# Linear attention's levels: differences two by two in place, none for the keys of the last level; later heads' weights get their low parts by a DMA that adds

## The chip, the cores and the metric

The kernel runs on one core of a Trainium2 chip. Work is spread over TensorE (PE, matrix products), VectorE (DVE), ScalarE (ACT), GpSimd (POOL) and the DMA queues, of which before the change SP's alone carries the data. The metric is the device time of one execution in microseconds (us); less is better.

## The reference, cut to what matters

The program is a backbone of two layers over 512 latent tokens and 256 context tokens (768 columns in all, `T`), width 1024. Each layer is a token mixer and a gated convolution MLP; layer 0's mixer is a bidirectional gated linear attention with 4 heads, key width 128 and value width 256, in chunks of 64 tokens:

```python
g = jax.nn.log_sigmoid((h @ a_w1[d]) @ a_w2[d] + a_b[d]) / GLA_GATE_NORM
...
b = jnp.cumsum(gc, axis=2)
b_last = b[:, :, -1:, :]
o_inter = jnp.einsum('bhid,bhde->bhie', qc * jnp.exp(b), s)
diff = jnp.where(mask, b[:, :, :, None, :] - b[:, :, None, :, :], -jnp.inf)
att = jnp.einsum('bhid,bhjd,bhijd->bhij', qc, kc, jnp.exp(diff))
o = o_inter + jnp.einsum('bhij,bhje->bhie', att, vc)
s_new = jnp.exp(b_last)[:, :, 0, :, None] * s + jnp.einsum('bhjd,bhje->bhde', kc * jnp.exp(b_last - b), vc)
```

`g` is the log of a decay for each token and key channel, `b` its running sum within a chunk. This is done forward and backward (over flipped tokens) and the two results are added, normalised, gated by `silu(r)` and projected.

## The kernel before, in words

Tokens lie along the free axis, 128 channels on the partitions; the chunk is 128 tokens here, six chunks (`CH`, `NCH`). A product in full fp32 is made of three faster ones (`mm3`, L294 to L297): both operands are split into a high part (rounded) and a low part (the rest), and low x high, high x low and high x high are added up in PSUM.

**Weights** come in units of 512 KB (`wunit`, L276). A load on SP's queue brings the unit into a staging tile `st` (a pool of three); ScalarE copies it into the high part `wh` (L290), which rounds it; VectorE subtracts for the low part `wl` (L291). `wh` and `wl` lie in a ring of five units. A head of the linear attention uses six: queries, keys, and four of values and gates together (`v` and `r`). A unit's ring place can be written once the matmuls of the unit five before it are done, and `st` is free when both parts are made.

**Decay inside a chunk.** The exponential of a difference of two running sums cannot be split safely into two factors over a whole chunk, so `level` (L560 on) halves the chunk seven times: `s` is 64, 32, ..., 1. Between the two halves of a block of 2s tokens the sum at the border is the reference point. `bF` and `bB` are the forward and backward running sums. L572 to L575 write four differences of half the columns each, one query tile `eq` and one key tile `ek`; L576 and L577 take the exponentials on ScalarE; L578 and L579 multiply by queries and keys; `blocks_of` (L550) makes the matmuls of the level (12 of 64 x 64 for the first, 24 of 32 x 32 for the later ones; the profile counts each twice), and a masked copy on VectorE (L588) or copies on ScalarE (L585) put the result into the attention tile. After the last level POOL copies four blocks (L592). `diag` (L558) is the block's own diagonal, from queries and keys alone.

**A head** has two parts. `part_a` is the first value group, the diagonal, and then the seven levels, with a value group (24 matmuls of 512 columns, `vr_group`) after each of the first five; between them, in heads 0 to 2, come 16 blocks of the modulation's weights (`sa`, 512 KB, two buffers, eight matmuls at L179 each). `part_b` is the decay of keys and queries (L600, L601, L634), their transposes (`kt`, L613), the states (L623, L628) and the outputs: the matmuls of L658, a square with its sum on ScalarE (L662), the root on POOL (`ms` L301, `rs` L303) and a scaled product on VectorE (L664, tiles `xl` and `xc`). Between these steps stand the next head's query and key projections (L515 copies them from PSUM), their rotation (L521 to L525; halves are swapped by small DMAs on SP's queue), and the gates (`gates_z`, `gates_b`: L480 to L496, where `b` is scanned).

**What sets the order.** The program is written head by head; a list scheduler puts each engine's instructions in an order by the place in the text and by modelled costs when the kernel is built. Each engine then runs its own list strictly in order. Tiles of 128 x 768 called `t` (`t3`) come from a pool of six.

Of the kernel before, what the change touches and what calls it, by code (L numbers as in the profile page):

```python
# [9 lines left out]
F32 = mybir.dt.float32  # L10
FR = mybir.dt.float32r
U8 = mybir.dt.uint8
AF = mybir.ActivationFunctionType
OP = mybir.AluOpType
# [6 lines left out]
HEADS = 4  # L21
# [18 lines left out]
def body(ctx, tc, x, ctx_x, small, ada0, ada, w_gla, a_w1, a_w2, w_go, w_fi, w_fo,  # L40
# [232 lines left out]
            o += b - a  # L273
        return out

    def wunit(src, eng=None, scales=None):  # L276


        n = src.shape[-1]
        st = wload(src)  # L280
        ring[0] = (ring[0] + 1) // 2 * 2 % NW
        (a, _), = wspans(2)
        hi, lo = (w[:, a:a + n] for w in WR)
        if scales:
            for i in range(2):
                s_, h_, l_ = (t_.rearrange("p (k i n) -> p k i n", i=2, n=128)[:, :, i, :] for t_ in (st, hi, lo))
                nc.scalar.activation(h_, s_, AF.Copy, scale=scales[i])
                nc.vector.scalar_tensor_tensor(l_, s_, scales[i], h_.bitcast(F32), OP.mult, OP.subtract)
            return hi, lo
        nc.scalar.activation(hi, st, AF.Copy)  # L290
        (eng or nc.vector).tensor_sub(lo, st, hi.bitcast(F32))  # L291
        return hi, lo

    def mm3(out, a, b, first, last, **at):  # L294
# [125 lines left out]

    Q_SCALE = 128.0 ** -0.5
    with tc.tile_pool(name="gla", bufs=6) as pool:
        def t3(dt=F32):
            return pool.tile([128, T], dt, name="t3", tag="t3", bufs=6)

        cosT = pool.tile([128, N_LAT], F32, name="cosT", bufs=1)
        sinT = pool.tile([128, N_LAT], F32, name="sinT", bufs=1)
# [44 lines left out]
        def gates_z(h):  # L472
            st[h]["g"] = []
            for d in range(2):
                e = t3()
                mn = t3()
                bias = sT[:, R_GB + 4 * d + h:R_GB + 4 * d + h + 1]
                for a, b in RNG:
                    ps = ps_aux()
                    mm(ps[:, 0:b - a], aw2[:, d, h * 128:(h + 1) * 128], low[d][:, a:b], start=True, stop=True)  # L480
                    nc.scalar.activation(e[:, a:b], ps[:, 0:b - a], AF.Abs, bias=bias)
                    nc.vector.tensor_scalar(mn[:, a:b], ps[:, 0:b - a], bias, 0.0, OP.add, OP.min)
                st[h]["g"].append((e, mn))
# [14 lines left out]
                st[h]["b"].append(bt)  # L498

        def qk_weights(h, i):  # L500
            st[h]["w", i] = wunit(w_gla[h, i])

        def qk_group(h, i, r):
            nm = "qk"[i]
            if r == 0:
                st[h][nm] = pool.tile([128, T], F32, name=nm, tag=nm, bufs=1)
            dst = st[h][nm]
            a, b = RNG[r]
            if h == 0:
                ps = groups[2 + 2 * i + r][2]  # L510
            else:
                wh, wl = (w.rearrange("p (k n) -> p k n", k=KD) for w in st[h]["w", i])
                ps = ps_mm()
                proj_fm(wh, wl, a, b, ps)
            nc.scalar.activation(dst[:, a:b], ps[:, 0:b - a], AF.Copy, scale=Q_SCALE if i == 0 else 1.0)  # L515

        def rope(h, i):
            dst = st[h]["qk"[i]]
            sw = t3()
            for o in (0, 64):  # L520
                nc.sync.dma_start(sw[o:o + 32, 0:N_LAT], dst[o + 32:o + 64, N_CTX:])  # L521
                nc.sync.dma_start(sw[o + 32:o + 64, 0:N_LAT], dst[o:o + 32, N_CTX:])
            nc.vector.tensor_mul(sw[:, 0:N_LAT], sw[:, 0:N_LAT], sinT)
            nc.vector.tensor_mul(dst[:, N_CTX:], dst[:, N_CTX:], cosT)
            nc.vector.tensor_add(dst[:, N_CTX:], dst[:, N_CTX:], sw[:, 0:N_LAT])  # L525

        def vr_weights(h, q):
            st[h]["wv", q] = wunit(w_gla[h, 2 + q])

        def vr_group(h, t):  # L530
            if h == 0:
# [28 lines left out]
        def level(h, li):  # L560
            s = LEVELS[li]
            n = T // (2 * s)
            bF, bB = st[h]["b"]

            def v(t_):
                return t_.rearrange("p (n two s) -> p n two s", two=2, s=s)

            cF = v(bF)[:, :, 0, s - 1:s].to_broadcast([128, n, s])
            cB = v(bB)[:, :, 1, 0:1].to_broadcast([128, n, s])
            eq = t3()  # L570
            ek = t3()
            nc.vector.tensor_sub(v(eq)[:, :, 1, :], v(bF)[:, :, 1, :], cF)  # L572
            nc.vector.tensor_sub(v(eq)[:, :, 0, :], v(bB)[:, :, 0, :], cB)
            nc.vector.tensor_sub(v(ek)[:, :, 0, :], v(bF)[:, :, 0, :], cF)
            nc.vector.tensor_sub(v(ek)[:, :, 1, :], v(bB)[:, :, 1, :], cB)  # L575
            nc.scalar.activation(eq, eq, AF.Exp, scale=1.0 / GATE)  # L576
            nc.scalar.activation(ek, ek, AF.Exp, scale=-1.0 / GATE)  # L577
            nc.vector.tensor_mul(eq, eq, st[h]["q"])  # L578
            nc.vector.tensor_mul(ek, ek, st[h]["k"])  # L579
            att, attd = st[h]["att"], st[h]["attd"]  # L580
            if s >= 32:
                ps = blocks_of(ek, eq, s, 1)
                for j in range(CH // s):
                    i = s * (j ^ 1)
                    nc.scalar.activation(att[s * j:s * j + s, :, i:i + s], ps[s * j:s * j + s], AF.Copy)  # L585
            else:
                ps = blocks_of(ek, eq, 32, 0)
                nc.vector.copy_predicated(attd, lvl[:, li - 2:li - 1, :].to_broadcast([128, NCH, 32]), ps)  # L588
            if s == 1:
                for j in range(4):  # L590
                    p_ = slice(32 * j, 32 * j + 32)
                    nc.gpsimd.tensor_copy(att[p_, :, p_], attd[p_])  # L592

        def key_decay(h, d):
            bt = st[h]["b"][d]
            last = ch(bt)[:, :, CH - 1:CH] if d == 0 else ch(bt)[:, :, 0:1]
            ed = sml.tile([128, NCH, 1], F32, name=f"ed{d}", tag=f"ed{d}", bufs=2)
            exps.append(nc.scalar.activation(ed, last, AF.Exp, scale=1.0 / GATE))
            kd = t3()
            nc.vector.tensor_sub(ch(kd), ch(bt), last.to_broadcast([128, NCH, CH]))  # L600
            exps.append(nc.scalar.activation(kd, kd, AF.Exp, scale=-1.0 / GATE))  # L601
            nc.vector.tensor_mul(kd, kd, st[h]["k"])
            st[h]["kd", d] = kd
            st[h]["ed", d] = ed

        def key_turn(h, d):
            kd = st[h].pop(("kd", d))
            kt = t3()
            for c0, c1 in ((0, 4), (4, 6)):
                ps = ps_aux()  # L610
                for c in range(c0, c1):
                    nc.tensor.transpose(ps[:, (c - c0) * CH:(c - c0 + 1) * CH], kd[:, c * CH:(c + 1) * CH], ident)
                nc.scalar.activation(kt[:, c0 * CH:c1 * CH], ps[:, 0:(c1 - c0) * CH], AF.Copy)  # L613
            st[h]["kt", d] = kt
            st[h]["S", d] = {}
# [13 lines left out]
            S[order[i + 1]] = s_new  # L629

        def query_decay(h):
            for d in range(2):
                e = t3()
                exps.append(nc.scalar.activation(e, st[h]["b"][d], AF.Exp, scale=1.0 / GATE))  # L634
                nc.vector.tensor_mul(e, e, st[h]["q"])
                st[h]["qd", d] = e
# [48 lines left out]
        def part_a(h, extra=None):  # L685
            vr_group(h, 0)
            diag(h)
            for i in range(7):
                level(h, i)
                todo = ada_step(pool, *blocks.pop(0)) if blocks and i < 6 else None  # L690
                if i < 5:
                    vr_group(h, i + 1)
                if todo:
                    todo()
                if extra and i >= 5:
                    extra(i - 5)

        def part_b(h, fill):

# [35 lines left out]
        def chain(*fs):  # L735
            def f():
                for g in fs:
                    g()
            return f
# [25 lines left out]
        for h in range(HEADS):  # L765
            part_a(h, turn_early if h == HEADS - 1 else None)
            n = h + 1
            if n < HEADS:
                qk_weights(n, 0)
                qk_weights(n, 1)  # L770
                part_b(h, [lambda: qk_group(n, 0, 0),
                           lambda: qk_group(n, 0, 1),
                           chain(lambda: rope(n, 0), lambda: qk_group(n, 1, 0)),
                           lambda: qk_group(n, 1, 1),
                           chain(lambda: rope(n, 1), lambda: gates_z(n)),
                           chain(lambda: gates_b(n), *[lambda q=q: vr_weights(n, q) for q in range(4)])])
            else:
                part_b(h, [lambda i=i: turn_early(i) for i in range(2, 7)])
        for t in (2, 3, 4, 5, 0, 1):
# [699 lines left out]
```

## Time and profile before

| | before |
|---|---|
| time, median of 3 runs | 1696.29 us (1695.89 to 1698.62) |
| profiled execution, its own time | 1698.42 us |
| span of the profiled execution | 1696.6 us |
| TensorE busy | 1643.0 us, 97% of the span |
| VectorE busy | 1173.5 us, 69% |
| ScalarE busy | 721.2 us, 43% |
| POOL busy | 175.0 us, 10% |
| mean granted TensorE clock | 0.994 of full speed |
| moved on SP's DMA queue | 177.97 MB |

Times in the views are us from the start of the span, durations ns. A row of a group has the source line, the engine, the operation, output and inputs, shapes, how many, then busy us and mean ns, then the idle time in front and what ended it. A row of waits has the waiting engine and line, what it waited for, and then us in total, times, and the longest. The linear attention takes about 80 to 392 us of the span.

### The profile page before, as it was taken

To read this page: it belongs to the slowest core of one execution; us is meant where nothing else is said; L and a number is where in the kernel's file an instruction comes from. 1 tells how busy PE (TensorE), PEld (TensorE's weight loads), DVE (VectorE), ACT (ScalarE), POOL (GpSimd) and SP (SyncE) were. 2 spreads that over 40 slices of the span, in tenths; PEclk is the share of its full clock that TensorE was granted. 3 is DMA by queue.
4 is the path that set the end of the run, shared out by engine and by line. 5 is a ranking of instruction groups with operands and counts; after the bars stand their busy time and mean duration, and the time that the engine had idled before them with its cause. 6 is when DMAs were issued, how large, how long until landed. Compare 5 with 4: busy or idle time off the path is not lost.

```text
span 1696.6 us, 27006 instructions
## 1 busy us (share of the span) xinstructions
PE 1643.0 (97%) x10867; PEld 1410.7 (83%) x10867; DVE 1173.5 (69%) x1949; ACT 721.2 (43%) x1265; POOL 175.0 (10%) x297
## 2 busy tenths in 40 slices
PE   5999999999999999999999999999998999999997
PEld 3768878778899998999999788888887888888887
DVE  4797777865997876978767665666668755555555
ACT  3655645553753343433425454434344422222232
POOL 1001010110000000000000043433332000000000
PEclk9999999999999999999999999999999999999999
DMA  7653523014233332524223043434331323322321
GB/s 268 189 176 100 175 75 107 20 51 144 93 125 112 112 112 75 163 74 146 78 87 100 1 132 93 126 112 131 95 114 53 95 92 100 98 89 75 112 88 50
DMA packets 54190, 179.70 MB, mean 106 GB/s; under 512 B 7024, under 2 KB 10864, under 8 KB 54064
## 3 DMA queue, kind: packets, MB, share of 16 engines
q1 hardware_dynamic: 54064, 177.97, 33.0%
q8 instruction: 85, 1.39, 0.3%
q14 instruction: 41, 0.34, 0.1%
HBM read 173.75 MB, written 2.10 MB: 104 GB/s over the span
## 4 chain that ended last, share of the span: by engine, by line
PE 84%; DVE 6%; ACT 4%; DMA 3%; issue 1%; POOL 1%; SPq 0%; POOLq 0%; DVEq 0%; ACTq 0%
PE mm L295 17%; PE mm L296 16%; PE mm L297 16%; PE aux L295 8%; PE aux L297 8%; PE aux L296 8%; PE mm L1259 2%; PE aux L1242 2%; DMA sa<-in 2%; PE aux L1217 2%; PE aux L658 1%; PE aux L623 1%; DMA st<-in 1%; PE aux L179 1%; PE mm L154 1%
## 5 line engine op out<-in xcount | busy, mean ns | idle before, releaser
L295 PE MATMUL mm<-hh,wl 128*128 128x512 f32 (+3 forms) x864 | 307.0, 358 | 5.0 <-ACT hh L379 2.5
L296 PE MATMUL mm<-hl,wh 128*128 128x512 f32 (+3 forms) x864 | 302.0, 350 | 0.3 <-DVE hl L308 0.3
L297 PE MATMUL mm<-hh,wh 128*128 128x512 f32 (+3 forms) x864 | 301.7, 350 | 0.0
L296 PE MATMUL mm<-ul,wh 128*128 128x512 f32 (+1 forms) x544 | 189.3, 348 | 0.3 <-DVE ul L308 0.3
L297 PE MATMUL mm<-uh,wh 128*128 128x512 f32 (+1 forms) x544 | 189.5, 349 | 0.0
L295 PE MATMUL mm<-uh,wl 128*128 128x512 f32 (+1 forms) x544 | 189.4, 350 | 0.0
L295 PEld LDWEIGHTS mm<-hh,wl 128*128 128x128 f32 (+1 forms) x864 | 162.8, 189 | 28.9 <-issue 5.1
L291 DVE TENSOR_TENSOR wl<-st,wh 128x1024 fp32r<-128x1024 f32 (+1 forms) x126 | 153.2, 1221 | 45.9 <-ACT wh L290 45.5
L290 ACT ACTIVATE wh<-st 128x1024 fp32r<-128x1024 f32 (+1 forms) x127 | 132.1, 1053 | 121.6 <-issue 69.6
L319 DVE SCALAR_TENSOR_TENSOR xl<-mm,mod,xl 128x512 f32<-128x512 f32 (+1 forms) x168 | 116.2, 698 | 95.0 <-PE mm L297 94.5
L296 PEld LDWEIGHTS mm<-hl,wh 128*128 128x128 f32 (+1 forms) x864 | 163.5, 189 | 18.4 <-issue 0.8
L297 PEld LDWEIGHTS mm<-hh,wh 128*128 128x128 f32 (+1 forms) x864 | 163.2, 189 | 18.3 <-issue 0.8
L295 PE MATMUL aux<-hh,wl 128*128 128x384 f32 (+2 forms) x496 | 174.0, 351 | 0.0
L296 PE MATMUL aux<-hl,wh 128*128 128x384 f32 (+2 forms) x496 | 173.7, 350 | 0.0
L297 PE MATMUL aux<-hh,wh 128*128 128x384 f32 (+2 forms) x496 | 173.7, 350 | 0.0
L270 ACT ACTIVATE wh<-st 128x512 fp32r<-128x512 f32 (+1 forms) x126 | 94.3, 756 | 165.9 <-issue 57.0
L295 PEld LDWEIGHTS mm<-uh,wl 128*128 128x128 f32 x544 | 103.0, 190 | 15.9 <-ACT uh L307 2.4
L296 PEld LDWEIGHTS mm<-ul,wh 128*128 128x128 f32 x544 | 103.2, 190 | 14.9 <-DVE ul L308 0.5
L271 DVE TENSOR_TENSOR wl<-st,wh 128x512 fp32r<-128x512 f32 (+1 forms) x126 | 104.6, 849 | 14.4 <-ACT wh L270 13.9
L297 PEld LDWEIGHTS mm<-uh,wh 128*128 128x128 f32 x544 | 103.0, 189 | 13.4
L355 POOL TENSOR_TENSOR rs<-ms,mhalf 128x2 f32<-128x2 f32 (+1 forms) x10 | 10.0, 1003 | 934.2 <-DVE ms L353 934.2
L295 PEld LDWEIGHTS aux<-hh,wl 128*128 128x128 f32 x496 | 93.7, 189 | 8.7 <-issue 1.4
(319 smaller groups left out, 3172.1 us busy)
## 6 DMA issues: line engine op xcount, KB each, us to landing
st<-in SPq DMA_DIRECT2D x201, 512.0 KB, 3.7
sa<-in SPq DMA_DIRECT2D x98, 512.0 KB, 3.7
sx<-in SPq DMA_DIRECT2D x14, 512.0 KB, 7.0
xl<-in SPq DMA_DIRECT2D x8, 512.0 KB, 5.8
xc<-in SPq DMA_DIRECT2D x4, 512.0 KB, 7.8
out<-y SPq DMA_DIRECT2D x16, 128.0 KB, 1.7
raw<-in SPq DMA_DIRECT2D x16, 96.0 KB, 2.5
t<-q SPq DMA_DIRECT2D x16, 64.0 KB, 2.0
```

The source lines that it names most:

```text
L154: mm(ps[32 * j:32 * j + 32, 256 * m:256 * m + 256], cs[:, 4 * half + j, :], st[:, j, :], start=half == 0, stop=half == 1, skip_group_check ...
L270: nc.scalar.activation(hi, s_, AF.Copy)
L271: nc.vector.tensor_sub(lo, s_, hi.bitcast(F32))
L290: nc.scalar.activation(hi, st, AF.Copy)
L291: (eng or nc.vector).tensor_sub(lo, st, hi.bitcast(F32))
L295: mm(out, a[1], b[0], start=first, stop=False, **at)
L296: mm(out, a[0], b[1], start=False, stop=False, **at)
L297: mm(out, a[0], b[0], start=False, stop=last, **at)
L319: nc.vector.scalar_tensor_tensor(x_, ps, gate(l, n, d, rng), x_, OP.mult, OP.add)
L1217: mm(pss[hh][:, off:off + 256], qe[a_][p_, 128 * t:128 * t + 128], ke[b_][p_, ks], start=i == 0, stop=i == 2)
L1242: nc.tensor.transpose(pT[:, i * 128:(i + 1) * 128], S2[:, o:o + 128], ident)
L1259: mm(po[64 * hh:64 * hh + 64, 128 * t:128 * t + 128], V[:, vs[i], 64 * hh:64 * hh + 64], PTs[hh][:, i * 128:(i + 1) * 128], start=i == 0, ...
```

## The change

Four edits, all of them in layer 0's linear attention:

1. Tiles of 128 x 768 are taken in pairs (`pair`): one tile of 128 x 1536, three buffers in place of six. The two halves are freed together.
2. In `level` the query and key tiles are the halves of one pair. For s above 1 one instruction writes both differences against the forward border (the second half of each block of `eq`, the first half of each block of `ek`), one both against the backward border: two of 768 columns for four of 384. For s = 1 a block's key is its own reference, so the key tile is `k` itself: no difference, exponential or product of keys.
3. For heads 1 to 3 the low part is made in another way: ScalarE copies `-st` into `wl` with rounding, and then a DMA on POOL's queue reads the weight again from memory and adds it to `wl`. Head 0 keeps the subtraction.
4. The next head's query and key weights are called for inside `part_a` (after the first and the sixth level) and not behind it; the four value units one by one in the first four gaps of `part_b`, and not all in the sixth.

```diff
--- before.py
+++ after.py
@@ -273,7 +273,7 @@
             o += b - a
         return out
 
-    def wunit(src, eng=None, scales=None):
+    def wunit(src, eng=None, scales=None, added=False):
 
 
         n = src.shape[-1]
@@ -288,7 +288,11 @@
                 nc.vector.scalar_tensor_tensor(l_, s_, scales[i], h_.bitcast(F32), OP.mult, OP.subtract)
             return hi, lo
         nc.scalar.activation(hi, st, AF.Copy)
-        (eng or nc.vector).tensor_sub(lo, st, hi.bitcast(F32))
+        if added:
+            nc.scalar.activation(lo, st, AF.Copy, scale=-1.0)
+            nc.gpsimd.dma_start(lo, src, accum_op=OP.add)
+        else:
+            (eng or nc.vector).tensor_sub(lo, st, hi.bitcast(F32))
         return hi, lo
 
     def mm3(out, a, b, first, last, **at):
@@ -420,8 +424,10 @@
 
     Q_SCALE = 128.0 ** -0.5
     with tc.tile_pool(name="gla", bufs=6) as pool:
-        def t3(dt=F32):
-            return pool.tile([128, T], dt, name="t3", tag="t3", bufs=6)
+        def pair():
+
+            t_ = pool.tile([128, 2 * T], F32, name="t2", tag="t2", bufs=3)
+            return t_, t_[:, 0:T], t_[:, T:2 * T]
 
         cosT = pool.tile([128, N_LAT], F32, name="cosT", bufs=1)
         sinT = pool.tile([128, N_LAT], F32, name="sinT", bufs=1)
@@ -472,8 +478,7 @@
         def gates_z(h):
             st[h]["g"] = []
             for d in range(2):
-                e = t3()
-                mn = t3()
+                _, e, mn = pair()
                 bias = sT[:, R_GB + 4 * d + h:R_GB + 4 * d + h + 1]
                 for a, b in RNG:
                     ps = ps_aux()
@@ -498,7 +503,7 @@
                 st[h]["b"].append(bt)
 
         def qk_weights(h, i):
-            st[h]["w", i] = wunit(w_gla[h, i])
+            st[h]["w", i] = wunit(w_gla[h, i], added=h > 0)
 
         def qk_group(h, i, r):
             nm = "qk"[i]
@@ -516,7 +521,9 @@
 
         def rope(h, i):
             dst = st[h]["qk"[i]]
-            sw = t3()
+            if i == 0:
+                st[h]["sw"] = pair()
+            sw = st[h]["sw"][1 + i]
             for o in (0, 64):
                 nc.sync.dma_start(sw[o:o + 32, 0:N_LAT], dst[o + 32:o + 64, N_CTX:])
                 nc.sync.dma_start(sw[o + 32:o + 64, 0:N_LAT], dst[o:o + 32, N_CTX:])
@@ -525,7 +532,7 @@
             nc.vector.tensor_add(dst[:, N_CTX:], dst[:, N_CTX:], sw[:, 0:N_LAT])
 
         def vr_weights(h, q):
-            st[h]["wv", q] = wunit(w_gla[h, 2 + q])
+            st[h]["wv", q] = wunit(w_gla[h, 2 + q], added=h > 0)
 
         def vr_group(h, t):
             if h == 0:
@@ -565,18 +572,23 @@
             def v(t_):
                 return t_.rearrange("p (n two s) -> p n two s", two=2, s=s)
 
-            cF = v(bF)[:, :, 0, s - 1:s].to_broadcast([128, n, s])
-            cB = v(bB)[:, :, 1, 0:1].to_broadcast([128, n, s])
-            eq = t3()
-            ek = t3()
-            nc.vector.tensor_sub(v(eq)[:, :, 1, :], v(bF)[:, :, 1, :], cF)
-            nc.vector.tensor_sub(v(eq)[:, :, 0, :], v(bB)[:, :, 0, :], cB)
-            nc.vector.tensor_sub(v(ek)[:, :, 0, :], v(bF)[:, :, 0, :], cF)
-            nc.vector.tensor_sub(v(ek)[:, :, 1, :], v(bB)[:, :, 1, :], cB)
+            cF, cB = v(bF)[:, :, 0, s - 1:s], v(bB)[:, :, 1, 0:1]
+            both, eq, ek = pair()
+            if s == 1:
+                nc.vector.tensor_sub(v(eq)[:, :, 1, :], v(bF)[:, :, 1, :], cF)
+                nc.vector.tensor_sub(v(eq)[:, :, 0, :], v(bB)[:, :, 0, :], cB)
+                ek = st[h]["k"]
+            else:
+
+
+                for c_, bt, first, second in ((cF, bF, T, s), (cB, bB, 0, T + s)):
+                    halves = bass.AP(both.tensor, both.offset + first,
+                                     [list(both.ap[0]), [2 * s, n], [second - first, 2], [1, s]])
+                    nc.vector.tensor_sub(halves, v(bt), c_[:, :, :, None].to_broadcast([128, n, 2, s]))
+                nc.scalar.activation(ek, ek, AF.Exp, scale=-1.0 / GATE)
+                nc.vector.tensor_mul(ek, ek, st[h]["k"])
             nc.scalar.activation(eq, eq, AF.Exp, scale=1.0 / GATE)
-            nc.scalar.activation(ek, ek, AF.Exp, scale=-1.0 / GATE)
             nc.vector.tensor_mul(eq, eq, st[h]["q"])
-            nc.vector.tensor_mul(ek, ek, st[h]["k"])
             att, attd = st[h]["att"], st[h]["attd"]
             if s >= 32:
                 ps = blocks_of(ek, eq, s, 1)
@@ -596,7 +608,9 @@
             last = ch(bt)[:, :, CH - 1:CH] if d == 0 else ch(bt)[:, :, 0:1]
             ed = sml.tile([128, NCH, 1], F32, name=f"ed{d}", tag=f"ed{d}", bufs=2)
             exps.append(nc.scalar.activation(ed, last, AF.Exp, scale=1.0 / GATE))
-            kd = t3()
+            if d == 0:
+                st[h]["kds"] = pair()
+            kd = st[h]["kds"][1 + d]
             nc.vector.tensor_sub(ch(kd), ch(bt), last.to_broadcast([128, NCH, CH]))
             exps.append(nc.scalar.activation(kd, kd, AF.Exp, scale=-1.0 / GATE))
             nc.vector.tensor_mul(kd, kd, st[h]["k"])
@@ -605,7 +619,9 @@
 
         def key_turn(h, d):
             kd = st[h].pop(("kd", d))
-            kt = t3()
+            if d == 0:
+                st[h]["kts"] = pair()
+            kt = st[h]["kts"][1 + d]
             for c0, c1 in ((0, 4), (4, 6)):
                 ps = ps_aux()
                 for c in range(c0, c1):
@@ -629,8 +645,9 @@
             S[order[i + 1]] = s_new
 
         def query_decay(h):
+            qds = pair()
             for d in range(2):
-                e = t3()
+                e = qds[1 + d]
                 exps.append(nc.scalar.activation(e, st[h]["b"][d], AF.Exp, scale=1.0 / GATE))
                 nc.vector.tensor_mul(e, e, st[h]["q"])
                 st[h]["qd", d] = e
@@ -694,6 +711,8 @@
                     todo()
                 if extra and i >= 5:
                     extra(i - 5)
+                if h < HEADS - 1 and i in (0, 5):
+                    qk_weights(h + 1, i // 5)
 
         def part_b(h, fill):
 
@@ -766,14 +785,12 @@
             part_a(h, turn_early if h == HEADS - 1 else None)
             n = h + 1
             if n < HEADS:
-                qk_weights(n, 0)
-                qk_weights(n, 1)
-                part_b(h, [lambda: qk_group(n, 0, 0),
-                           lambda: qk_group(n, 0, 1),
-                           chain(lambda: rope(n, 0), lambda: qk_group(n, 1, 0)),
-                           lambda: qk_group(n, 1, 1),
+                part_b(h, [chain(lambda: qk_group(n, 0, 0), lambda: vr_weights(n, 0)),
+                           chain(lambda: qk_group(n, 0, 1), lambda: vr_weights(n, 1)),
+                           chain(lambda: rope(n, 0), lambda: qk_group(n, 1, 0), lambda: vr_weights(n, 2)),
+                           chain(lambda: qk_group(n, 1, 1), lambda: vr_weights(n, 3)),
                            chain(lambda: rope(n, 1), lambda: gates_z(n)),
-                           chain(lambda: gates_b(n), *[lambda q=q: vr_weights(n, q) for q in range(4)])])
+                           lambda: gates_b(n)])
             else:
                 part_b(h, [lambda i=i: turn_early(i) for i in range(2, 7)])
         for t in (2, 3, 4, 5, 0, 1):
```

In the order of TensorE at head 2's first level (L550 in the old text, L557 in the new) the rows before are, from the queries' and keys' diagonal on, with the matmuls of the first value group between:

```order
L550 MATMUL aux<-q,k 32x32 x24
...
L297 MATMUL mm<-wh,hh 128x512
L550 MATMUL aux<-t_2469,t_2470 64x64 x12
L179 MATMUL aux<-sa,cs 32x256 x8
L295 MATMUL mm<-wh,hl 128x512
```

and now:

```order
L557 MATMUL aux<-q,k 32x32 x24
...
L299 MATMUL mm<-wh,hl 128x512
L557 MATMUL aux<-t_2420 64x64 x12
L179 MATMUL aux<-sa,cs 32x256 x8
L557 MATMUL aux<-t_2488 32x32 x24
L300 MATMUL mm<-wl,hh 128x512
```

The second level follows on the first. Counted from the last gate projection (`low`), 51 value matmuls stood before the 64 x 64 ones in head 2 and 61 stand there now; in head 1 it was 48 and is 60, in head 3 52 and 59, in head 0 68 and 75.

In the order of VectorE at the same place (head 2; `b_...` are the two running sums, `t_2469` and `t_2470` the first level's query and key tiles, `t_2535` the second level's) the rows before are:

```order
L558 TENSOR_TENSOR attd<-aux,two_i 128x192
L572 TENSOR_TENSOR t_2469<-b_2365 128x6x64
L573 TENSOR_TENSOR t_2469<-b_2370 128x6x64
L574 TENSOR_TENSOR t_2470<-b_2365 128x6x64
L575 TENSOR_TENSOR t_2470<-b_2370 128x6x64
L572 TENSOR_TENSOR t_2535<-b_2365 128x12x32
L578 TENSOR_TENSOR t_2469<-t_2469,q 128x768
L579 TENSOR_TENSOR t_2470<-t_2470,k 128x768
L573 TENSOR_TENSOR t_2535<-b_2370 128x12x32
```

and now, where `t_2420` and `t_2488` are the first and the second level's pairs:

```order
L565 TENSOR_TENSOR attd<-aux,two_i 128x192
L587 TENSOR_TENSOR t_2420<-b_2332 128x6x2x64
L587 TENSOR_TENSOR t_2420<-b_2337 128x6x2x64
L587 TENSOR_TENSOR t_2488<-b_2332 128x12x2x32
L587 TENSOR_TENSOR t_2488<-b_2337 128x12x2x32
L589 TENSOR_TENSOR t_2420<-t_2420,k 128x768
L591 TENSOR_TENSOR t_2420<-t_2420,q 128x768
L589 TENSOR_TENSOR t_2488<-t_2488,k 128x768
L591 TENSOR_TENSOR t_2488<-t_2488,q 128x768
```

Both differences of the second level now stand ahead of the first level's products; it was one of four.

In POOL's list between the attention tile's copies of head 0 and the outputs of that head stood:

```order
L592 COPY att<-attd 32x6x32 x4
L301 TENSOR_SCALAR ms<-ss 128x1
L303 TENSOR_TENSOR rs<-ms,mhalf 128x1
```

and now:

```order
L293 DMA wl<-in 128x1024 x3
L604 COPY att<-attd 32x6x32 x4
L293 DMA wl<-in 128x1024 x2
L305 TENSOR_SCALAR ms<-ss 128x1
L307 TENSOR_TENSOR rs<-ms,mhalf 128x1
L293 DMA wl<-in 128x1024
```

Adding transfers for the next head stand ahead of these copies and between the pairs of the root.

## The prediction

> **What bounds the kernel now.** I first read the page's totals, then the table of windows over the linear attention (roughly 80 to 392 us; the rest of the program keeps its instructions in order), then what TensorE waits for there.
>
> ```profile
> span 1696.6 us, 27006 instructions
> PE 1643.0 (97%) x10867; PEld 1410.7 (83%) x10867; DVE 1173.5 (69%) x1949; ACT 721.2 (43%) x1265; POOL 175.0 (10%) x297
> ```
>
> ```profile
> 100.00:120.00 20.00, 18.29 (x295) 10.94 (x293) 16.97 (x29) 10.14 (x15) 0.00 (x0) 1.00 0.71 216
> ...
> 200.00:220.00 20.00, 19.85 (x158) 18.85 (x157) 7.76 (x15) 10.61 (x23) 2.95 (x8) 1.00 0.48 152
> ...
> 240.00:260.00 20.00, 17.18 (x217) 11.26 (x216) 19.38 (x36) 11.80 (x21) 0.00 (x0) 1.00 0.42 132
> ...
> 320.00:340.00 20.00, 19.14 (x238) 14.95 (x237) 20.00 (x37) 12.64 (x23) 0.00 (x0) 1.00 0.01 2
> ```
>
> Each row gives a stretch's ends and length, the busy us of TensorE, its weight loads, VectorE, ScalarE and POOL with their instructions, TensorE's granted clock, the DMA engines' busy share and GB/s. TensorE sets the end. VectorE is full while a head's seven levels run (19.38 and 20.00 of 20 us), and still TensorE is at 17 to 19 us there; where the next head is projected VectorE has 12 us in 20 to spare. VectorE work is worth something only where TensorE waits for it:
>
> ```profile
> PE aux L179 <- DMA sa<-in: 3.5, 6, 1.4
> PE aux L550 <- DVE t L579: 2.9, 3, 1.1
> PE aux L671 <- DVE xl L664: 1.4, 2, 0.7
> PE aux L623 <- DVE xl L664: 1.2, 3, 0.4
> PE aux L550 <- DVE k L525: 1.0, 1, 1.0
> PE aux L658 <- DVE xl L664: 1.0, 2, 0.5
> PE aux L671 <- DVE xc L664: 0.5, 1, 0.5
> PE aux L623 <- ACT t L613: 0.3, 1, 0.3
> ```
>
> These are all of TensorE's waits between 80 and 392 us, 11.8 us in sum: 3.5 for the modulation weights `sa`, 8.3 for VectorE and ScalarE. That caps any gain from this change near 12 us, 0.7% of the time. The three waits on L579 are the first level of heads 1, 2 and 3; later levels wait for nothing, since a value group stands between them on TensorE.
>
> **The change part by part.** *Fewer instructions on VectorE.* The prices:
>
> ```profile
> L579 DVE TENSOR_TENSOR t<-t,k 128x768 f32<-128x768 f32 x28 | 26.8, 956 | 1.1 <-ACT t L577 1.0
> ...
> L577 ACT ACTIVATE t<-t 128x768 f32<-128x768 f32 x28 | 23.7, 846 | 4.2 <-DVE t L575 3.1
> ...
> L291 DVE TENSOR_TENSOR wl<-st,wh 128x1024 fp32r<-128x1024 f32 x18 | 21.8, 1224 | 16.0 <-ACT wh L290 15.6
> ...
> L290 ACT ACTIVATE wh<-st 128x1024 fp32r<-128x1024 f32 x18 | 19.0, 1066 | 4.2 <-PE mm L297 2.5 <-DMA st<-in 1.7
> ...
> L600 DVE TENSOR_TENSOR t<-b 128x768 f32<-128x768 f32 x8 | 7.4, 952 | 0.0
> ```
>
> The timeline of VectorE at head 1's first level shows that these durations overlap by about 0.08 us, so the distance from start to start is the real cost:
>
> ```profile
> 163.21 0.35 DVE L558 TENSOR_TENSOR attd<-aux,two_i 128x192 f32<-128x192 f32 x1
> 163.47 0.55 DVE L573 TENSOR_TENSOR t<-b 128x384 f32<-128x384 f32 x1
> 163.93 0.56 DVE L574 TENSOR_TENSOR t<-b 128x384 f32<-128x384 f32 x1
> 164.40 0.55 DVE L575 TENSOR_TENSOR t<-b 128x384 f32<-128x384 f32 x1
> 164.87 0.55 DVE L572 TENSOR_TENSOR t<-b 128x384 f32<-128x384 f32 x1
> 165.34 0.95 DVE L578 TENSOR_TENSOR t<-t,q 128x768 f32<-128x768 f32 x1
> 166.21 0.95 DVE L579 TENSOR_TENSOR t<-t,k 128x768 f32<-128x768 f32 x1
> ```
>
> A half-width difference costs 0.47 us, a full-width operation 0.87. The new differences are 768 wide with a broadcast operand, like L600, so 0.87 each is my value; were their four-dimensional pattern to cost nothing extra or as much as the two halves it replaces, the bounds are 0.87 and 0.94. Six levels of a head go from 4 x 0.47 = 1.88 to 2 x 0.87 = 1.74, which is only 0.14 us each; the last level loses 2 x 0.47 + 0.87 = 1.81 and one exponential of 0.85 on ScalarE. For four heads: 24 x 0.14 + 4 x 1.81 = 10.6 us. The 18 differences of the weights' low parts take away 18 x 1.14 = 20.5 more. About 31 us leave VectorE, but nearly all under cover of TensorE's own work: the weights' part lies where VectorE was idle, the levels' part behind the first level, where TensorE does not wait. If that cover were gone, those 31 us would count; the cap above says it is not.
>
> *The first level of heads 1 to 3.* Here two things move. The order now has 60, 61 and 59 value-projection matmuls between a head's gate projection and its first level's matmuls, where it had 48, 51 and 52: 12, 10 and 7 more in front, and in head 1 seven more modulation ones. One stands 0.23 us behind the other:
>
> ```profile
> 164.35 0.39 PE L296 MATMUL mm<-wl,hh 128*128 128x512 f32 x1
> 164.58 0.39 PE L297 MATMUL mm<-wh,hh 128*128 128x512 f32 x1
> ...
> 165.58 0.62 PE L179 MATMUL aux<-sa,cs 128*32 128x256 f32 x2
> 167.22 0.92 PE L550 MATMUL aux<-t,t 128*64 128x64 f32 x24 [1.02 <-DVE t L579]
> ```
>
> So TensorE comes to the first level about 2.8, 2.3 and 1.6 us later (that only moves work it has to do anyhow). On VectorE the first level's chain gets longer, though: between the diagonal and the second product there stand two (head 1: one) full-width differences of its own, two of the *next* level's, and two products. In head 1 that is 0.26 + 5 x 0.87 + 0.08 = 4.7 us from L558 to the end, against 167.16 - 163.21 = 3.95; in heads 2 and 3 it is 5.6 against 4.4 (one half-width difference more than head 1 had). The waits shrink by the differences, as far as they last: all of head 1's 1.0 (2.8 - 0.7 leaves 2.1), 1.1 in head 2 (2.3 - 1.2) and 0.4 in head 3 (1.6 - 1.2). Sum **-2.5 us**, bounds -2.9 (all three waits) and 0: ScalarE puts two copies of a finished value group (0.4 us each) and one weight pass ahead of head 1's gates, which could eat head 1's part.
>
> *ScalarE.* It gets 18 more passes over a weight at L290's price, 18 x 1.06 = 19.1 us, and loses 4 x 0.85: +15.7 us. ScalarE is at 10 to 13 us of 20 in the windows above, so this fits; what counts is who queues behind. In each of heads 0 to 2 one pass stands ahead of the second key copy and waits for the same projection, so keys, their rotation swap and the copies behind come 1.06 us later. The output chain (square on ScalarE, root on POOL, L664 on VectorE) is what 4.1 us of the waits above end on. A pass ahead of such a square would cost up to 1.06 us, in three heads 3.2. Against that VectorE reaches L664 sooner, having no 1.14 us difference in front of it. I take **+0.5 us**, from -1 to +3.
>
> *The adding DMAs.* 18 transfers of 512 KB go out on POOL's queue. No row shows such a transfer; the nearest are loads of the same size:
>
> ```profile
> st<-in SPq DMA_DIRECT2D x201, 512.0 KB, 3.7
> ...
> xc<-in SPq DMA_DIRECT2D x4, 512.0 KB, 7.8
> ```
>
> An add reads a source and its destination and writes once; 3.7 to 7.8 us bounds it, and I take 6. What must be met, in head 2 on the clock of before:
>
> ```profile
> 206.13 1.09 ACT L290 ACTIVATE wh<-st 128x1024 fp32r<-128x1024 f32 x1
> ...
> 211.26 1.05 ACT L290 ACTIVATE wh<-st 128x1024 fp32r<-128x1024 f32 x1
> 225.71 0.40 PE L296 MATMUL mm<-wl,hh 128*128 128x512 f32 x1
> ...
> 230.54 0.40 PE L296 MATMUL mm<-wl,hh 128*128 128x512 f32 x1
> ```
>
> The middle value weights have high parts at 207 and 212; with one more pass each the adds leave by about 208 and 214, and the first low part is needed at 225.7, the third one's around 230.5. That leaves 16 us for one transfer and some 6 us each if four run one after the other, so I cost this at **0**. The cover is the key projection; without it each head would wait the whole transfer, 3 x 6 = 18 us. On POOL four copies of the attention tile and the ms/rs pairs queue behind adds that wait for ScalarE's pass; the copies are needed some 10 us after they are made, an ms/rs pair at once (in the 0.5 above). [...]
>
> *Modulation weights in head 0.* Their loads go round two buffers, and the chain that ended last runs through them:
>
> ```profile
> 99.67 5.41 DMA sa<-in
> ...
> 105.82 3.88 DMA sa<-in
> ...
> 110.44 4.49 DMA sa<-in
> ...
> 115.68 4.47 DMA sa<-in
> ```
>
> A buffer is asked for again only when TensorE has used it. In the new order the first use stands 7 value matmuls later (1.6 us), with two weight loads ahead of the ring on SP's queue. The ring takes the same time after that, with 1.6 us less work to fill it: **+1.2 us**, bounds 0 (head 0 was not late everywhere) and +3 (a load of 3.7 us in between). The paired tiles use the same memory; released two by two they cost 0 unless a stage waits for a pair, bound 1 us.
>
> Sum: -2.5 + 0.5 + 0 + 1.2 = -0.8 us on the profiled execution's 1698.42, and an estimated -1 (one 1.14 us difference) where L664 and the state updates no longer queue behind weight differences in gaps that the view does not name: **-1.8 us**, 1696.6 on that execution. It lies 2.1 us above the median of the three, 1696.29, so on the median the forecast is **1694.5 us**: within 0.2% (3.4 us), which is about what a measurement of this kernel can tell from no change.
>
> **Rivals.** *All VectorE waits go* (0.37): the seven kinds of wait other than `sa` end, 8.3 us: 1688.0, or enough of them to come under 1692.9. For it: VectorE is relieved at every place named. Against: the L664 waits end on POOL's root, which nothing shortens.
>
> *The ring takes the whole gain* (counted with the forecast's 0.42): -2.5 + 3 gives 1696.8; the change then does what it says and moves only which wait ends last.
>
> *The adds come late* (0.14, slower): each of heads 1 to 3 starts its value group on a low part that has not landed. It decides from 16 us for one or 6 us each in a row. At 8 us each, from 208 on, the third lands at 232, 1.5 us late, and the fourth at 240, needed another 4.8 us after the third (as far apart as 225.7 and 230.5): 4.7 late. Some 3 us per head: 1694.5 + 9 = 1703.5. For it: 0.71 of the DMA engines' time is taken in 100 to 120 us. Against: 0.48 where head 2 is fed.
>
> [...]
>
> **Numbers.** Forecast with the ring 0.42, all waits gone 0.37, late adds 0.14, descriptors 0.07. Faster by over 0.2% (below 1692.9): 0.37. Within 0.2% (1692.9 to 1699.7): 0.42. Slower, the last two cases: 0.21. The likeliest case's own range is 1692.9 to 1698; to hold 8 in 10 it must reach most of the second case and the start of the slow ones: 1686 to 1701.
>
> **What would show it.** In the profile after: L550's waits on the second product under 1 us in sum (step one); the new differences at 0.95 us, 0.87 apart; ScalarE about 16 us busier; TensorE's wait for `sa` up by 1 to 2 us; no wait of L295 or L296 on a DMA at the start of a head's value group. I am wrong if TensorE waits there for a low part, if its sum of waits between 80 and 392 us falls under 6 us (more gain) or rises over 15 (a loss), or if the part after 400 us moves.

## The result and the profile after

The changed kernel takes **1715.49 us** (median of 5, 1712.07 to 1716.69) where the kernel before, on the same chip, takes 1696.29: ratio **1.0103**, 95% interval 1.0092 to 1.0114. It is slower by 1%, where 1694.5 us was predicted. The profiled execution took 1712.07 us.

The page of the changed kernel, its totals, DMA queues and DMA issues (size of one, median us from issue to landing):

```profile
span 1710.3 us, 26970 instructions
PE 1647.9 (96%) x10867; PEld 1409.8 (82%) x10867; DVE 1142.3 (67%) x1871; ACT 731.1 (43%) x1279; POOL 188.3 (11%) x315
...
q1 hardware_dynamic: 54064, 177.97, 31.9%
q0 software_dynamic: 2592, 9.44, 3.0%
...
st<-in SPq DMA_DIRECT2D x201, 512.0 KB, 3.7
...
wl<-in POOLq DMA_DIRECT2D x18, 512.0 KB, 7.8
```

VectorE lost 31.2 us (1173.5 to 1142.3), just what was worked out, and yet the profiled execution got 13.7 us longer than the one before (19.2 by the medians). What TensorE waited for most in the linear attention, now 80 to 410 us:

```profile
PE aux L179 <- DMA sa<-in: 6.6, 7, 3.7
PE aux L485 <- DVE xc L681: 2.6, 2, 2.0
PE aux L557 <- DVE t L591: 2.3, 3, 1.0
PE aux L639 <- DVE xl L681: 2.1, 3, 0.9
PE aux L485 <- DVE S L644: 1.9, 3, 1.0
```

All its waits there come to 20.2 us, where they were 11.8; the prediction had named over 15 as a sign that it is wrong. No value-group matmul waits for a low part: the adding transfers are in time for their own readers. Instead modulation weights come 3.7 us late once, and the gate projection (L485) waits for VectorE, which it never did before. Where this happens shows in the chain of waits between 104 and 154 us (start, us, what):

```profile
106.85 4.33 DMA sa<-in
...
111.93 7.50 DMA sa<-in
119.43 0.04 issue
119.48 1.08 PE aux L179 x8
...
141.41 8.89 DMA t<-q
```

and what POOL did then, in its timeline:

```profile
111.93 0.87 POOL L293 DMA_DIRECT2D wl<-in  x1 [28.42 <-ACT wl L292]
118.40 0.86 POOL L293 DMA_DIRECT2D wl<-in  x1 [5.60 <-ACT wl L292]
...
136.16 0.86 POOL L293 DMA_DIRECT2D wl<-in  x1 [6.68 <-ACT wl L292]
138.04 0.86 POOL L293 DMA_DIRECT2D wl<-in  x1 [1.02 <-ACT wl L292]
```

An adding transfer is issued and a modulation load starts in the same hundredth of a microsecond, 111.93, and the load takes 7.5 us where those before it in the ring take 4.3 to 4.8. At 136 to 142 us three more adds go out with weight loads, and a swap of 64 KB, 2.0 us before, lands after 8.9 us. VectorE, in order, stands at the rotation (L530) and behind it wait the output's scaling (L681) and the states (L644), whose PSUM buffers the gate projection needs.

There is a second cost behind these two stalls. Two windows of the changed kernel, columns as in the prediction, then its TensorE timeline around the two pauses:

```profile
120.00:140.00 20.00, 19.87 (x208) 16.96 (x201) 4.40 (x7) 15.97 (x29) 4.57 (x8) 0.93 0.63 182
140.00:160.00 20.00, 17.43 (x80) 15.25 (x79) 6.45 (x12) 3.83 (x7) 3.10 (x5) 0.91 0.83 205
```

```profile
119.48 1.08 PE L179 MATMUL aux<-sa,cs 128*32 128x256 f32 x8 [3.69 <-DMA sa<-in]
...
121.51 0.63 PE L301 MATMUL mm<-wh,hh 128*128 128x512 f32 x1
121.93 0.63 PE L299 MATMUL mm<-wh,hl 128*128 128x512 f32 x1
...
152.17 0.45 PE L485 MATMUL aux<-low,aw 96*128 96x384 f32 x1 [2.03 <-DVE xc L681]
153.16 0.44 PE L485 MATMUL aux<-low,aw 96*128 96x384 f32 x1 [0.54 <-DVE S L644]
...
155.29 0.63 PE L300 MATMUL mm<-wl,hh 128*128 128x512 f32 x1
155.72 0.63 PE L301 MATMUL mm<-wh,hh 128*128 128x512 f32 x1
```

Behind both pauses the matmuls stand 0.42 to 0.43 us apart, not 0.23, for about 3 us; the granted clock of the two windows is 0.93 and 0.91 (1.00 before). That is up to 20 x 0.07 + 20 x 0.09 = 3.2 us.

By head, from its first 64 x 64 matmul to the next head's, the changed kernel needs 87.3, 79.7 and 79.9 us; without the adding transfers and with nearly the same order on TensorE (the second run below) it is 77.4, 77.7 and 79.0. So 9.9 of the loss lie between the first levels of heads 0 and 1, 2.0 and 0.9 behind. Of the 9.9, 5.5 are named waits (9.2 in sum against 3.7) and some 3 the slow clock; about 1 us has no name.

### The profile page after: what moved, and what is told of

Its sections match the earlier page's. It is cut to its first block, busy times and chain, and to the rows that moved or that the text cites. A ratio compares the mean times of both kernels' runs of the same rounds, so it can differ in the third digit from the quotient of the medians.

```text
span 1710.3 us, 26970 instructions
## 1 busy us (share of the span) xinstructions
PE 1647.9 (96%) x10867; PEld 1409.8 (82%) x10867; DVE 1142.3 (67%) x1871; ACT 731.1 (43%) x1279; POOL 188.3 (11%) x315
## 3 DMA queue, kind: packets, MB, share of 16 engines
q1 hardware_dynamic: 54064, 177.97, 31.9%
## 4 chain that ended last, share of the span: by engine, by line
PE 76%; DVE 8%; ACT 6%; DMA 6%; issue 2%; POOL 1%; SPq 1%; POOLq 0%; DVEq 0%; ACTq 0%
PE mm L299 15%; PE mm L301 15%; PE mm L300 15%; PE aux L299 7%; PE aux L301 7%; PE aux L300 7%; DMA sa<-in 2%; PE mm L1276 2%; PE aux L1259 2%; PE aux L1234 2%; DMA t<-q 1%; DMA st<-in 1%; ACT wh L290 1%; PE aux L675 1%; DVE wl L271 1%
## 5 line engine op out<-in xcount | busy, mean ns | idle before, releaser
L295 DVE TENSOR_TENSOR wl<-st,wh 128x1024 fp32r<-128x1024 f32 (+1 forms) x108 | 132.0, 1227 | 28.8 <-ACT wh L290 28.3
```

## The experiments

Each ratio is against runs of the kernel before on the same chip in the same session (medians 1698.5 to 1699.2 us there).

**e1: the same instructions, an eighth of the bytes.**

```diff
-            nc.gpsimd.dma_start(lo, src, accum_op=OP.add)
+            nc.gpsimd.dma_start(lo[:, 0:128], src[:, 0:128], accum_op=OP.add)
```

> The changed kernel with every instruction and every engine's order kept, but each adding transfer carries 128 of its 1024 columns (64 KB, not 512 KB); the rest of the low part stays the negated weight, so the weights of heads 1 to 3 are computed wrong and only the time counts. Theory traffic (the 512 KB adding transfers take DMA engine time from the modulation loads in head 0 and from the 64 KB rotation swaps, whose landing went from 2.0 to 8.4 us): the 7.5 us load and the 8.9 us swap go back to about 4.5 and 2 us, TensorE's waits in 95 to 160 us fall by 6 to 9 us, and the time is 1697 to 1703. Theory ScalarE and order (the 18 extra passes ahead of the query copies, and the new order): nothing of that leaves, 1710 to 1716.

1702.65 us, ratio 1.0024 (1.0012 to 1.0037): three quarters of the loss are gone with the bytes alone, the order of the engines unchanged but for two neighbouring matmuls on TensorE. In its waits and DMA issues between 80 and 410 us:

```profile
PE aux L179 <- DMA sa<-in: 5.0, 11, 1.1
```

```profile
wl<-in POOLq DMA_DIRECT2D x18, 64.0 KB, 4.9
...
t<-q SPq DMA_DIRECT2D x12, 64.0 KB, 5.6
```

No wait is over 1.1 us and none is left at the gate projection. The swaps did not go back to 2 us, though: on SP's queue two weight loads now stand right ahead of them, perhaps since `st` comes free later with ScalarE's second pass (not tested). At 5.6 us they do no harm.

**e2: no adding transfers at all**; the low parts come from VectorE, everything else as changed.

```diff
-            st[h]["w", i] = wunit(w_gla[h, i], added=h > 0)
+            st[h]["w", i] = wunit(w_gla[h, i])
...
-            st[h]["wv", q] = wunit(w_gla[h, 2 + q], added=h > 0)
+            st[h]["wv", q] = wunit(w_gla[h, 2 + q])
```

> The changed kernel with the low parts of all heads by VectorE's subtraction again; pairs, levels and the new place of the weights stay. Traffic or ScalarE at fault: 1692 to 1698. Order at fault (weights called for earlier, value matmuls ahead of the first level): 1706 to 1715.

1700.22 us, ratio 1.0014 (1.0003 to 1.0024). The adding transfers are nearly all of the loss; but the other three edits, which should have gained, do not.

**e3: only the adding transfers**, put into the kernel before (edit 3 of the change alone).

> The kernel before with only the adding transfers and their ScalarE passes in heads 1 to 3. Traffic: between 1704 and 1714, with swaps over 5 us. Order or levels at fault: within 4 us of the kernel before.

1711.25 us, ratio 1.0077 (1.0062 to 1.0092), as the traffic theory had it: a wait of 3.9 us for `sa`, swaps of 7.2 us. The order of the change is not needed for most of the loss.

**e4: only the pairs and the levels** (edits 1 and 2 in the kernel before).

> The kernel before with only the pairs and the new levels. My prediction's terms for these alone (first-level waits -2.5, ring about +1) give 1693 to 1697. If the levels or pairs are at fault: 1703 or more.

1701.62 us, ratio 1.0016 (1.0002 to 1.0030). My own terms, tested alone, missed: no gain, 0.0016 lost.

**e5, e6, e7: which of the transfers.** Head 1 subtracted and heads 2 and 3 added; only the value units added; only the query and key units added.

```diff
-            st[h]["w", i] = wunit(w_gla[h, i], added=h > 0)
+            st[h]["w", i] = wunit(w_gla[h, i], added=h > 1)
```

> The changed kernel with head 1's low parts by VectorE's subtraction; heads 2 and 3 still add by DMA. From the traces the adding transfers cost about 10 us on the way to head 1's first level and 2.1 and 0.9 us in the two stages behind. So if the loss sits where they meet the modulation ring and head 1's swaps, this is 1700 + 3 = 1703; if each head's six transfers cost alike (15 us / 3), 1710.

> Only the four value units of heads 1 to 3 add by DMA; the query and key units are subtracted on VectorE. The value units' transfers leave beside the rotation swaps. If the swap is the half of the loss that the trace shows (waits of 3.2 us at the gate projection, 1.5 us at half speed, and 3 us in heads 2 and 3): 1706 to 1709, swaps still over 6 us, no wait for modulation over 1.5 us. If the modulation ring is all of it: 1700 to 1702.

> The other way round: only the query and key units add by DMA, and these leave beside head 0's modulation loads. If the ring is the half that the trace shows (3.9 us more waiting and 1.9 us at half speed): 1705 to 1708, a modulation load over 7 us, swaps back at about 2 us. If the swap is all of it: 1700 to 1702.

1708.65 (1.0059, 1.0038 to 1.0080), 1716.09 (1.0093, 1.0074 to 1.0113) and 1710.08 (1.0064, 1.0047 to 1.0081). e5 came near its second case, every head alike; e6 and e7 fell outside both of theirs, although the long modulation load and the swaps at about 2 us that e7's first case named did come. Against e2's 1.0014, heads 2 and 3 cost about 0.0045, some 7.6 us, and head 1 the other half (1.0103 - 1.0059): more even than the stages of one trace said. The split by units did not split ring from swap: in e6 the first two value units' adds left at 116.6 and 118.0 us, into the ring. The two halves alone cost 9 and 13 us (by the same ratios), more than the 15 of both; a stall of the ring of 5 us comes with either, as the chain of waits shows, e7 first, then e6:

```profile
113.19 8.88 DMA sa<-in
```

```profile
118.34 10.03 DMA sa<-in
```

What e7 says for itself: with swaps at 2.1 us, the loss over e2 is still some 8.5 us. Most of it goes with the ring: its waits for `sa` are 8.4 us in sum against 3.2 in e2, and the granted clock over 110 to 130 us is 0.83, 3.4 us lost.

**e8: the same transfers, not adding.**

```diff
-            nc.gpsimd.dma_start(lo, src, accum_op=OP.add)
+            nc.gpsimd.dma_start(lo, src)
```

> The changed kernel with its 18 transfers on POOL's queue kept in size and place, but copying the weight over the low part in place of adding to it, so heads 1 to 3 get wrong weights. In the page one adding transfer takes 3.0% of 1710 us over 18, 2.85 us of all 16 engines; a plain load of the same size 31.9% over 339.5, 1.61 us. If the engines' time is what is short, this gives back some half of the loss: 1704 to 1709. If only the number of bytes or of transfers counts: 1712 to 1716. If the adding itself is at fault (and plain transfers of 512 KB hide): 1699 to 1702.

1707.03 us, ratio 1.0052 (1.0035 to 1.0069): half of the loss is left, as the engines' time has it. What went are the waits at the gate projection (4.5 us in sum to 0.2); a stall of 3.2 us for `sa` stays. From its page:

```profile
q0 software_dynamic: 2592, 9.44, 1.8%
...
wl<-in POOLq DMA_DIRECT2D x18, 512.0 KB, 5.2
```

1.8% of 1705.1 us over 18 is 1.71 us of all 16 engines for a transfer; the adding one took 3.0% of 1710.3, 2.85. By these figures adding costs some 1.7 times the engines' time of copying.

**e10: the same adds at another time**, the key unit's and the first value unit's held until POOL has made the attention copies.

```diff
+            late = lambda: behind([nc.gpsimd.dma_start(lo, src, accum_op=OP.add)], copies)
+            late_adds.append(late) if added == 2 else late()
```

> The changed kernel with all its adding transfers, the query/key and value ones of the next head held back behind the copies of the attention tile on POOL, that is until a head's modulation loads are done (in head 0 from 112 and 118 us to about 129). Same bytes, other time. If meeting in time is the cause, the modulation load of 7.5 us is back at 4.5, TensorE's 3.9 us stall and the slow 2 us behind it go, and the time is 1706 to 1711, with swaps as late as before or later. If the adding transfers cost by their number wherever they stand: 1713 to 1717.

1713.08 us, ratio 1.0079 (1.0063 to 1.0095). The mechanism was hit: those two adds leave together at 125.7 us, none of head 0's loads takes over 5.6, no wait for `sa` is over 1.1 us, the granted clock is 1.00 from 100 to 200 us, and the stage between heads 0 and 1 falls from 87.3 to 81.5 us. The total gained less than that (0.0024 of ratio, 4 us), and the time lies where the second case had it. The swaps are as late as they were, 8.4 us in the changed kernel; from the DMA issues of e10:

```profile
wl<-in POOLq DMA_DIRECT2D x18, 512.0 KB, 8.2
...
t<-q SPq DMA_DIRECT2D x12, 64.0 KB, 8.6
```

The waits at the gate projection are 2.8 and 2.1 us, against 2.6 and 1.9. In head 2 they are now followed by a lower granted clock, 0.83 over 10 us,

```profile
230.00:240.00 10.00, 7.81 (x25) 5.39 (x24) 5.01 (x10) 1.80 (x5) 1.65 (x3) 0.83 0.60 138
```

and the stage between heads 1 and 2 takes 81.8 us in place of 79.7. Moved out of the one neighbour's way, the transfers still meet the other.

**e11: the swaps on ScalarE's queue.**

```diff
-                nc.sync.dma_start(sw[o:o + 32, 0:N_LAT], dst[o + 32:o + 64, N_CTX:])
+                nc.scalar.dma_start(sw[o:o + 32, 0:N_LAT], dst[o + 32:o + 64, N_CTX:])
```

> The changed kernel with the 64 KB rotation swaps issued on ScalarE's queue and not on SP's, where two 512 KB weight loads are issued right ahead of them. If the swaps are late because the 16 engines are full with adding transfers: swaps stay over 6 us, 1712 to 1717. If they are late because they stand in SP's queue behind those loads: swaps at 2 to 4 us, the 3.2 us wait at head 1's gate projection goes, 1706 to 1711.

1722.13 us, ratio 1.0131 (1.0112 to 1.0150), slower than either case had it; the swaps, now alone on their queue, still take

```profile
t<-q ACTq DMA_DIRECT2D x12, 64.0 KB, 7.4
```

That is the median of three heads, and they differ. The windows in which head 1's and head 2's four were issued (the last three columns are clock, DMA share and GB/s):

```profile
144.00:148.00 4.00, 4.00 (x21) 3.56 (x20) 0.88 (x2) 2.26 (x7) 0.61 (x2) 1.00 0.16 42
231.00:235.00 4.00, 4.00 (x25) 4.00 (x24) 0.48 (x1) 0.56 (x3) 0.77 (x3) 1.00 1.01 246
```

Head 1's landed in 2.0 us, with the engines busy 0.16 of the time; head 2's in 7.4, with three adds and three weight loads in flight and the engines full. So in this run a queue of their own does not free the swaps; what goes with their lateness is the full engines. The order also moved in this run, so its total is no price of the queue.

**e9: the first level's chain cut by 1.7 us**, in e2's kernel.

```diff
-                    nc.vector.tensor_sub(halves, v(bt), c_[:, :, :, None].to_broadcast([128, n, 2, s]))
+                    diff = nc.vector.tensor_sub(halves, v(bt), c_[:, :, :, None].to_broadcast([128, n, 2, s]))
+                    if li == 1:
+                        behind([diff], products)
```

> The changed kernel without the adding transfers (as in the second run: 1700.2 us, waits for the first levels' second product 2.9 us), with the second level's two differences put behind the first level's two products on VectorE. My prediction said the first level's chain had grown by the two full-width differences of the next level. If that is why the -2.5 us did not come: the chain is 1.7 us shorter, TensorE comes 4 value matmuls (0.9 us) sooner, the waits fall to under 1 us, and the time is 1697 to 1699. If the waits have another cause (the gates' chain ahead): waits stay over 2.5 us, 1700 to 1702.

1701.61 us, ratio 1.0020 (1.0009 to 1.0031), waits of 3.4 us in sum: the theory fell. A candidate stands earlier. In e2 the first gate instruction of head 2 on ScalarE, and the same in e12:

```profile
233.13 1.05 ACT L486 ACTIVATE t<-aux,sT 128x384 f32<-128x384 f32 x2 [2.06 <-DVE k L532]
```

```profile
224.18 1.04 ACT L486 ACTIVATE t<-aux,sT 128x384 f32<-128x384 f32 x2
```

In e2 it waits for the rotation of the keys (L532): the gates need a pair, and the rotation holds one of the three until its second half is done.

**e12, e13, e14: a tile of its own for the rotation**, in e2's kernel; with e9's shorter chain; with the weights called for where they were.

```diff
-            if i == 0:
-                st[h]["sw"] = pair()
-            sw = st[h]["sw"][1 + i]
+            sw = pool.tile([128, N_LAT], F32, name="sw", tag="sw", bufs=1)
```

> The changed kernel without the adding transfers, and with the rotation's swapped halves in a tile of their own (128 x 512) and not in a pair of the pool of three. In the run without adding transfers ScalarE's first gate instruction of head 2 waited until 233.1 us for the rotation of the keys, which holds the pair; before the change it ran at 224.0. If the pairs are why the levels bring nothing: that instruction runs within 2 us of its projection again, the waits at the first levels fall under 2 us in sum, and the time is 1695 to 1698 (the run without adding transfers: 1700.2). If pairs are not the cause: 1699 to 1702.

> The same, and the second level's differences behind the first level's products. If with early gates the first level's own chain is what TensorE waits for: 1 to 2 us less than the run before it, 1694 to 1697. If something ahead of it sets the time still: the same as it within 1 us.

> The kernel before with the new levels and pairs and the swapped halves in their own tile; the weights are called for where they were. If the earlier call for the weights costs nothing, the same as the first of these three within 1 us; if it costs the 1 us of the ring, 1 us less.

1700.40 (1.0008, 0.9998 to 1.0018), 1699.41 (1.0008, 0.9997 to 1.0018) and 1700.65 us (1.0009, 0.9999 to 1.0018), where the kernel before took 1698.93 in the same session: no difference that can be told from the kernel before, nor among the three. The gates are early again, and yet in e12:

```profile
PE aux L555 <- DVE t L589: 4.2, 4, 1.8
```

Three of these four waits, 3.8 us, are first levels. The list scheduler put the first levels 41 to 46 value matmuls behind the last gate projection, where e2 had 57 and 58 and the kernel before some 50. In nine traces (before, after, e1, e2, e9, e10, e12 to e14) the first level of each of heads 1 to 3 waits 0.4 to 2.0 us. With the gates early the place moved and the wait stayed; that the scheduler moved it because its model knew of the early gates is likely, not shown. None of the fourteen kernels came out faster than the one before.

## Why the prediction was wrong, point by point

- **The adding DMAs at 0** is the step that failed. Its check was whether the low parts come in time for their own readers, and they do, though one transfer took 5.6 to 11.3 us (median 7.8) and so half of them passed the upper bound of 7.8. What was not costed is the time of the shared 16 engines: 18 x 2.85 = 51 us of them, set between modulation loads that TensorE already waited for (3.5 us) and swaps that the rotation waits for. I had quoted 0.71 of the engines' time at 100 to 120 us and used it against the adds' own deadline alone. e1, e3 and e8 show it: with an eighth of the bytes 1.0024, the transfers alone 1.0077, without the adding 1.0052. In e1, e8 and the changed kernel, whose orders agree, the transfers take 0.6, 1.8 and 3.0% of the engines' span, some 10, 31 and 51 us, and the ratios are 0.0010, 0.0038 and 0.0089 above e2's. Engine time alone does not give the price, though: e7's six transfers took 1.1% and came out 0.0050 above e2. What they meet counts too, as e10 shows.
- **The ring at +1.2, bound +3.** Between the first levels of heads 0 and 1 the `sa` waits are 1.7 us before and 2.1 with no adds (e2): +0.4, so the later first use cost less than I took. With adds they are 4.9, +3.2; the bound, one load of 3.7 us in between, was about that size, but left out the lower clock behind the stall (0.93 in 120 to 140 us).
- **The rival of late adds** had the direction, but by the wrong mechanism (nothing waits for an add) and 12 us short (1703.5).
- **The case of descriptors (0.07)** took VectorE's work to hold up POOL's transfers, which no run shows. The issuing of an add on POOL takes 0.85 to 1.07 us and follows its releaser; the one at 82.44 us took 1.07 with VectorE busy 20.00 of 20 us in 80 to 100. From issue to landing the transfers took 7.8 us adding and 5.2 plain (medians), beside other traffic, where 6 had been taken.
- **First levels at -2.5** came as -0.6 (2.9 to 2.3 us) and as 0 in e2. I took the 7 to 12 value matmuls in front as a cover; by e12, where their number fell with early gates and the wait did not, they look like the scheduler's answer to a longer chain. The longer chain had a part that I priced at 0, a stage that waits for a pair: the gates behind the keys' rotation. With that undone (e12) the waits stay all the same, so the term was wrong in kind.
- **VectorE's 31 us under cover**: right, 31.2, and worth nothing, as said. The -1 us for L664 did not come either: TensorE's waits on its result are 4.1 us in sum before, 5.1 in e2. The new differences cost 0.951 us, 0.87 apart, as taken from L600.
- **ScalarE at +15.7** measured +9.9: the passes add 15.7 us (731.1 against e2's 715.4) and not 19.1, in part because passes of 1.07 us stand 0.95 us apart when they follow each other, and e2 is 5.8 us under before where 3.4 was priced. Its +0.5 us cannot be told apart: e1, which has all its passes, is 1.0010 over e2 with overlapping intervals.

What stays open: e5 to e7 do not add up, and how the loss divides between ring, swaps and the clock in the total time was not settled; only the trace's stages give it, for one execution. A version with both neighbours kept clear was not tried. Why the levels and pairs bring no gain is open too: undoing the early pair (e12) changed the time by nothing that can be told.

## What to carry to other kernels

The work that was moved here from VectorE to a DMA was not free, although its own reader never waited: 18 adds of 2.85 us of the engines took the ratio from 1.0014 to 1.0103. So ask which transfers run on the same engines at that moment, and which of them something waits for, the small ones above all (the swaps went from 2.0 to 8.4 us). Where a list scheduler places the work, a count of instructions standing in front of a waiting one may be its guess of lateness and not a cover. Buffers joined in pairs are held by the later of the two users: look for a stage that takes one early, as the gates of head 2 do, which began at 233.1 us in e2 and at 224.2 with a tile of its own for the rotation (e12), though that by itself bought no time.

## What was not expected of the hardware

An adding transfer of 512 KB takes 2.85 us of all 16 DMA engines, a copy on the same queue 1.71, and what moved on SP's queue, 31.9% of 1710.3 us over 339.5 such sizes, 1.61. In the changed kernel the pause of TensorE of 3.7 us before 119.48 us was followed by about 3 us with matmuls 0.43 us apart in place of 0.23. Pauses broken by one matmul are less plain: 2.0 and 0.5 us in the changed kernel were followed by the same 0.43 us (granted clock 0.91 in 140 to 160 us), 1.3 and 0.6 us at head 2 in e10 by a clock of 0.83 in 230 to 240 us, 2.2 and 0.55 us at head 1 in e10 by matmuls 0.23 us apart and a clock of 1.00. No run here shows what decides.
